# First mixer's projections as matmuls of 512 and 256 columns, halves joined by adding transfers, convolution taps one chunk later

## The chip, the cores and the metric

The kernel runs on one core of one Trainium2 chip, in one launch. Its time is the device time of that core in microseconds (us); a kernel is known by the median of its runs. Engines are named as the profile names them: PE is TensorE (PEld its weight loads), ACT is ScalarE, DVE is VectorE, POOL is GpSimd, SP is SyncE, which only issues transfers here.

## What is computed

The reference is a decoder trunk of two layers over 256 tokens of width 1024. Layer 0 mixes tokens with a Mamba-2 block (SSD), layer 1 with block attention; each is followed by a layer norm, a product-key expert mixer (PEER) over 16384 experts, another layer norm and a gated embedding add. The change is in the first mixer alone. What matters of it:

```python
def ssd_mixer(x, w_in, conv_w, conv_b, dt_bias, a_log, d_skip, norm_g, w_out):
    zxbcdt = x @ w_in                      # 256 x 5152
    z   = zxbcdt[..., :2048]
    xbc = zxbcdt[..., 2048:5120]
    dt  = zxbcdt[..., 5120:]
    xbc = silu(causal_depthwise_conv(xbc, conv_w, conv_b))   # 4 taps along the tokens
    xs, b_in, c_in = xbc[..., :2048], 4 groups of 128, 4 groups of 128
    ...                                    # chunked scan over two chunks of 128 tokens
    gated = y * silu(z)                    # per group of 512 channels
    gated = gated * rsqrt(mean(gated ** 2) + 1e-5)
    return (gated * norm_g) @ w_out
```

All of it is float32, and products are wanted at float32's precision.

## The kernel before

**Products from halves.** A float32 operand is split into a high part that the matrix unit takes exactly and the low rest: ACT writes the high part (`L124`, a cast of 128x1024), DVE the rest (`L125`, a subtraction of the same size). A product then needs three matmuls: high by high, high by low, low by high. `mm3` (`L145` to `L149`) issues these three, each with 256 columns where the tokens move.

**The first mixer's chunks.** The weights come in chunks of 128 output channels: 24 chunks of `w_xbc` (per group g: B, C, four of x), 16 of `w_z`, and 16 chunks of `w_so` for the output. A chunk is a transfer of 512 KB into one of four `raw` buffers, issued by SP, then the cast and the subtraction into one of four `hl` buffers, then the matmuls. `stationary` (`L151`) runs a chunk of `w_xbc` or `w_z` as 8 x 3 matmuls of 256 columns into a PSUM bank of the tag `mm`, of which there are two. The first six chunks of `w_z` are plain float32 matmuls (`L419`) from the unsplit weights and need neither ACT nor DVE first.

**The convolution.** After a chunk of `w_xbc`, `conv` copies the PSUM bank to `cv_raw` on ACT (`L395`), writes `cv_y` as bias plus the last tap on ACT, also from PSUM (`L396`), adds three shifted taps on DVE (`L399`), and applies SiLU on ACT (`L400`). A chunk of `w_z` is copied to `z` (`L423`); SiLU over the four chunks of a group follows later (`L428`).

**The other form of the product, already used elsewhere.** `halves` (`L156` to `L162`) lays the high and the low tokens side by side: a high weight tile meets both in one matmul of 512 columns, whose two halves of the bank are joined afterwards, and a low weight tile meets the high tokens in one of 256. So a chunk has 8 matmuls of each kind; with `turned` the two kinds of weight tile alternate in reversed order, so that two matmuls of one width follow each other. The expert mixer uses it for all 128 chunks of `u`: two ACT copies out of the bank (`L916`, `L917`), and POOL issues a transfer that adds the second copy onto the first (`L918`, 128 KB); the activation that reads the sum comes three to seven chunks later in the program.

**What sets the order.** Each engine runs its own list of instructions in order; a wait at the head of a list holds back everything behind it. The lists are made when the kernel is built, by a scheduler that takes what it holds to be ready, within edges: `after(marks)` keeps an instruction behind a given one on the same engine, and `weave` hands out side work between the chunks. In the first mixer the chunks come as: groups 0 and 1 of `w_xbc` (12 chunks), groups 0 and 1 of `w_z` (8, six of them plain), group 2 of `w_xbc` and the output chunks of group 0, group 3 of `w_xbc` and group 2 of `w_z`, group 3 of `w_z`, the other output chunks. The scan of a group (`ssd_mix`: `L442` to `L518`) and its norm (`L528` to `L540`, where POOL adds squares, `L536`, and takes a root, `L553`) run as side work beside the chunks of later groups.

Of the kernel before, what the change touches and what calls it, by code (L numbers as in the profile page):

```python
# [11 lines left out]
AF = mybir.ActivationFunctionType  # L12
OP = mybir.AluOpType
# [4 lines left out]
P = 128  # L18
T = 256
D = 1024  # L20
KD = D // P
# [19 lines left out]
P_CONVW, P_CONVB, P_D, P_NG, P_LN, P_ALOG, P_DTB, P_END = 0, 96, 120, 136, 152, 216, 248, 280  # L41
# [25 lines left out]
class Net:  # L67
# [88 lines left out]
    def halves(self, out, hl, ks=range(KD), turned=False):  # L156
        o = out.rearrange("p (b t) -> p b t", b=2)
        order = [(k, a) for k in ks for a in ((1, 0) if turned and k % 2 else (0, 1))]
        for k, a in order:
            dst, src = ((o, self.xT[:, :, k, :]), (out[:, :T], self.xT[:, 0, k, :]))[a]  # L160
            self.nc.tensor.matmul(dst, hl[:, a, k * P:(k + 1) * P], src, start=k + a == 0,  # L161
                                  stop=(k, a) == order[-1] and k == KD - 1)  # L162

    def moving(self, out, hl, xk, first, last, c=slice(0, 512)):
        for k in range(2):
# [103 lines left out]
    def ssd(self):  # L269
        nc, dram = self.nc, self.dram  # L270
        with self.tc.tile_pool(name="ssd", bufs=1) as pool:
# [12 lines left out]
            nc.sync.dma_start(self.tri, dram["consts"][:, C_TRI:C_ALIBI])  # L284
            x = pool.tile([P, 2, D], F32, name="xn")
            self.grp, self.zs, self.ns, self.ys, self.ac, self.ce, self.sq, self.rs = ({} for _ in range(8))
            self.last = []
            ins = [self.ssd_in(g) for g in range(4)]
            zs = [self.ssd_z(g) for g in range(4)]
            ssm = [self.ssd_mix(g) for g in range(4)]  # L290
# [96 lines left out]

    def conv(self, dst, hl, c):
        nc, prm = self.nc, self.params
        pc = self.mm()  # L390
        self.stationary(pc[:, :T], hl)
        raw = self.tl([P, T], "cv_raw", 2)
        y = self.tl([P, T], "cv_y", 2)
        w = lambda k: prm[:, P_CONVW + 4 * c + k:P_CONVW + 4 * c + k + 1]
        nc.scalar.copy(raw, pc[:, :T])  # L395
        nc.scalar.activation(y, pc[:, :T], AF.Identity, bias=prm[:, P_CONVB + c:P_CONVB + c + 1], scale=w(3))  # L396
        for k in range(3):
            d = 3 - k
            nc.vector.scalar_tensor_tensor(y[:, d:], raw[:, :T - d], w(k), y[:, d:], op0=OP.mult, op1=OP.add)  # L399
        self.last_silu = nc.scalar.activation(dst, y, AF.Silu).ins  # L400

    def ssd_in(self, g):
        def step(j):
# [7 lines left out]
    def ssd_z(self, g):  # L411
        def step(j):
            if j == 0:
                self.zs[g] = self.tl([P, 4, T], "z", 2)
            pz = self.mm()
            if 4 * g + j in PLAIN:
                raw = self.plain(self.dram["w_z"][4 * g + j])
                for k in range(KD):
                    self.nc.tensor.matmul(pz[:, :T], raw[:, k * P:(k + 1) * P], self.xT32[:, k, :],  # L419
                                          start=k == 0, stop=k == KD - 1)  # L420
            else:
                self.stationary(pz[:, :T], self.chunk(self.dram["w_z"][4 * g + j]))
            self.nc.scalar.copy(self.zs[g][:, j, :], pz[:, :T])  # L423
        return [lambda j=j: step(j) for j in range(4)]

    def ssd_silu(self, g):
# [128 lines left out]
    def ssd_out(self, g, x):  # L555
        def step(kp, h):
            hl = self.chunk(self.dram["w_so"][(2 * g + kp) * 2 + h])
            if kp + h == 0:
                self.oacc = self.accs()
            if g == 3:  # L560
                self.last.append((h, kp, hl, (0, 1)))
                return
            for tb in range(2):
                acc = self.oacc[tb][h]
                self.moving(acc, hl, lambda a, k: self.ns[g][:, a, 2 * kp + k, tb * P:(tb + 1) * P], kp == 0, kp == 1)
                if kp:
                    v = x[:, tb, h * 512:(h + 1) * 512]
                    self.nc.vector.scalar_tensor_tensor(v, acc, self.rs[g][:, tb:tb + 1], v, op0=OP.mult, op1=OP.add)
        return [lambda kp=kp, h=h: step(kp, h) for kp in range(2) for h in range(2)]
# [873 lines left out]
```

## Time and profile before

| | us |
|---|---|
| median of 3 runs | 1862.36 |
| lowest and highest of them | 1859.06, 1872.17 |
| the profiled execution's own time | 1860.15 |
| its span, first to last instruction | 1858.3 |
| PE busy in the span | 1819.4 (98%) |
| DVE busy | 1490.3 (80%) |
| ACT busy | 1151.4 (62%) |
| POOL busy | 635.7 (34%) |

The first mixer takes the first 207 us of the span; the expert mixer of layer 0 begins at 207.35 us. The busy figures are unions over the whole program, whose stages have different limits, so the prediction reads the stretches of the first mixer one by one. In a row of the timeline the first number is the start, the second the length of a run of like instructions, and the bracket tells how long the engine had been idle and who released it. Instructions on one engine overlap a little (the next starts some 0.1 us before the last one's end), so the cost of one in a row of many is read from start to start.

### The profile page before, as it was taken

The page shows a single profiled execution, that of the slowest core. Times are in us where ns is not written, and L with a number is a line of the kernel's source. Part 1 is how long each engine was busy: PE and PEld are TensorE (multiplying, and loading weights), DVE is VectorE, ACT ScalarE, POOL GpSimd, SP SyncE. Part 2 cuts the span into 40 slices and gives each one's busy share as a digit, 9 for nine tenths or more (in the row PEclk, how much of TensorE's full clock was granted, in tenths as well). Part 3 has the DMA queues.
Part 4 walks back from the last instruction along what each step waited for, and adds up shares of the span by engine and source line. Part 5 has one row for each costly group of instructions (what it writes and reads, how often), then busy time and mean ns, then how long its engine had stood idle before and what let it go on. Part 6 is the DMA issues. An engine that isn't in the chain of part 4 may idle for free. (4 is left out here: it accounts for less than half of the span.)

```text
span 1858.3 us, 31744 instructions
## 1 busy us (share of the span) xinstructions
PE 1819.4 (98%) x11112; PEld 1542.1 (83%) x11112; DVE 1490.3 (80%) x2936; ACT 1151.4 (62%) x2330; POOL 635.7 (34%) x620
## 2 busy tenths in 40 slices
PE   9999999999999999999999999999999999999998
PEld 8998888888888877787788788888888887777777
DVE  7798789989989986666667778998998998666656
ACT  6865456696666666555546655669666665555553
POOL 0001013332222257787700001323222225777671
PEclk9999999999999999999999999999999999999999
DMA  7555669897699998889736556989779999888871
GB/s 270 202 186 185 217 178 228 218 243 200 183 275 334 286 313 289 282 291 338 247 107 195 187 195 191 228 217 254 189 185 285 331 288 297 274 279 284 315 238 60
DMA packets 217904, 444.29 MB, mean 239 GB/s; under 512 B 18980, under 2 KB 126664, under 8 KB 216072
## 3 DMA queue, kind: packets, MB, share of 16 engines
q1 hardware_dynamic: 75208, 266.75, 42.8%
q0 software_dynamic: 67648, 137.66, 28.6%
q10 hardware_dynamic: 74880, 37.75, 7.0%
q8 instruction: 91, 1.49, 0.3%
q14 instruction: 77, 0.63, 0.1%
HBM read 364.46 MB, written 44.08 MB: 220 GB/s over the span
## 5 line engine op out<-in xcount | busy, mean ns | idle before, releaser
L125 DVE TENSOR_TENSOR hl<-raw,hl 128x1024 fp32r<-128x1024 f32 x570 | 694.0, 1220 | 205.4 <-ACT hl L124 150.1
L161 PE MATMUL acc<-xT,hl 128*128 128x256 f32 (+1 forms) x4608 | 841.2, 340 | 1.6 <-DVE xT L188 0.8
L161 PEld LDWEIGHTS acc<-xT,hl 128*128 128x128 f32 x4608 | 700.7, 188 | 101.8 <-DVE hl L125 4.2
L124 ACT CAST hl<-raw 128x1024 fp32r<-128x1024 f32 x570 | 597.8, 1052 | 217.2 <-PE acc L149 69.7
L149 PE MATMUL acc<-hl,w 128*128 128x512 f32 x2220 | 529.6, 399 | 27.4 <-issue 9.5
L149 PEld LDWEIGHTS acc<-hl,w 128*128 128x128 f32 x2220 | 423.2, 192 | 132.5 <-issue 18.4
L918 POOL DMA_DIRECT2D w<-w x160 | 139.3, 870 | 399.1 <-ACT w L937 236.5
L918 POOL DMA_DIRECT2D act<-w x96 | 83.7, 872 | 303.6 <-ACT w L917 182.4
L1172 POOL DMA_INDIRECT raw<-in_v,r x136 | 157.9, 1161 | 62.0 <-issue 36.2
L916 ACT COPY w<-acc 128x256 f32<-128x256 f32 x160 | 59.9, 374 | 160.3 <-PE acc L161 156.6
L1172 POOL DMA_INDIRECT rows_w<-w_d,r x122 | 140.0, 1148 | 37.2 <-issue 35.0
L149 PE MATMUL mm<-xT,hl 128*128 128x256 f32 x816 | 100.8, 284 | 0.2 <-DVE hl L125 0.2
L149 PEld LDWEIGHTS mm<-xT,hl 128*128 128x128 f32 x816 | 98.5, 192 | 1.5 <-issue 0.9
L917 ACT COPY w<-acc 128x256 f32<-128x256 f32 x256 | 97.4, 380 | 0.0
L962 DVE TENSOR_TENSOR pick<-pick,r 128x2048 f16<-128x2048 f16 x64 | 78.2, 1222 | 1.0
L978 PEld LDWEIGHTS <-pick 128*128 128x128 f16 x1024 | 67.1, 98 | 13.1 <-issue 9.7
L916 ACT COPY act<-acc 128x256 f32<-128x256 f32 x96 | 35.7, 371 | 66.9 <-PE acc L161 66.4
L979 PE MATMUL mm<-pick 128*128 128x96 f16 x512 | 67.5, 206 | 0.0
L214 POOL TENSOR_TENSOR ln_s<-ln_s,mhalf 128x1 f32<-128x1 f32 x8 | 4.4, 552 | 177.2 <-PE acc L149 130.5
L536 POOL TENSOR_TENSOR sq<-sq,sqt 128x256 f32<-128x256 f32 x12 | 12.5, 1041 | 150.3 <-ACT sqt L535 150.1
L978 PE MATMUL aux<-pick 128*128 128x128 f16 x688 | 59.3, 220 | 0.3
L125 DVE TENSOR_TENSOR hl<-pick,hl 128x1024 fp32r<-128x1024 f32 x32 | 39.2, 1224 | 25.4 <-ACT hl L124 18.9
(290 smaller groups left out, 2118.0 us busy)
## 6 DMA issues: line engine op xcount, KB each, us to landing
raw<-in_u SPq DMA_DIRECT2D x256, 512.0 KB
raw<-in_v SPq DMA_DIRECT2D x64, 512.0 KB
w_d<-act ACTq DMA_DIRECT2D x48, 512.0 KB
w<-w POOLq DMA_DIRECT2D x160, 128.0 KB
raw<-in_w_q SPq DMA_DIRECT2D x32, 512.0 KB
raw<-in_w_xbc SPq DMA_DIRECT2D x24, 512.0 KB
act<-w POOLq DMA_DIRECT2D x96, 128.0 KB
a_d<-act ACTq DMA_DIRECT2D x24, 512.0 KB
```

Source lines behind the costliest of these rows:

```text
L124: a = self.nc.scalar.copy(hi, src)
L125: b = self.nc.vector.tensor_tensor(lo, src, hi.bitcast(F32), op=OP.subtract)
L149: self.last_mm = self.nc.tensor.matmul(out, lhs(a), rhs(b), start=start and i == 0, stop=stop and i == 2).ins
L161: self.nc.tensor.matmul(dst, hl[:, a, k * P:(k + 1) * P], src, start=k + a == 0, stop=(k, a) == order[-1] and k == KD - 1)
L536: nc.gpsimd.tensor_tensor(self.sq[g], self.sq[g], t, op=OP.add)
L916: nc.scalar.copy(whole, pe[:, :T])
L917: copied = nc.scalar.copy(pair[:, 1, :], pe[:, T:]).ins
L918: nc.gpsimd.dma_start(whole, pair[:, 1, :], accum_op=OP.add)
L962: nc.vector.tensor_tensor(a2, both, gates, op=OP.mult)
L978: nc.tensor.matmul(pg[:, t, :], one[:, 0, 4 * h + t], a2[:, 4 * h + t, k], start=k == 0, stop=k == 1)
L979: nc.tensor.matmul(banks["used"][:, MANY * tb:MANY * tb + MANY], one[:, 0, 4 * h + t], a2[:, 4 * h + t, 0, :MANY], start=at == 0, stop=at ...
L1172: got = nc.gpsimd.indirect_dma_start(out=dst, out_offset=None, in_=src, in_offset=rows(which))
```

## The change

Four things change, in the first mixer only.

- The 24 chunks of `w_xbc` and the 10 chunks of `w_z` that are not plain go through `halves` in its turned order: 16 matmuls (8 of 512 columns, 8 of 256) in place of 24 of 256.
- The two halves of the bank are joined as in the expert mixer (`joined`): one ACT copy of the first half into its place (`cv_raw` or `z`), one of the second into a new tile `low`, and a transfer issued by POOL that adds `low` onto it.
- Bias and last tap (`cv_y`) now read `cv_raw` in SBUF, after that transfer, and not PSUM.
- The rest of the convolution of a chunk (`finish`) is put off until after the next chunk's copies: `flush` issues it behind `self.copied`, the last ACT copy. `cv_raw` has three buffers in place of two, `low` has three.

```diff
     def conv(self, dst, hl, c):
         nc, prm = self.nc, self.params
-        pc = self.mm()
-        self.stationary(pc[:, :T], hl)
-        raw = self.tl([P, T], "cv_raw", 2)
-        y = self.tl([P, T], "cv_y", 2)
+        raw = self.tl([P, T], "cv_raw", 3)
+        self.joined(raw, hl)
         w = lambda k: prm[:, P_CONVW + 4 * c + k:P_CONVW + 4 * c + k + 1]
-        nc.scalar.copy(raw, pc[:, :T])
-        nc.scalar.activation(y, pc[:, :T], AF.Identity, bias=prm[:, P_CONVB + c:P_CONVB + c + 1], scale=w(3))
-        for k in range(3):
-            d = 3 - k
-            nc.vector.scalar_tensor_tensor(y[:, d:], raw[:, :T - d], w(k), y[:, d:], op0=OP.mult, op1=OP.add)
-        self.last_silu = nc.scalar.activation(dst, y, AF.Silu).ins
+
+        def finish():
+            y = self.tl([P, T], "cv_y", 2)
+            nc.scalar.activation(y, raw, AF.Identity, bias=prm[:, P_CONVB + c:P_CONVB + c + 1], scale=w(3))
+            for k in range(3):
+                d = 3 - k
+                nc.vector.scalar_tensor_tensor(y[:, d:], raw[:, :T - d], w(k), y[:, d:], op0=OP.mult, op1=OP.add)
+            self.last_silu = nc.scalar.activation(dst, y, AF.Silu).ins
+
+        self.flush()
+        self.pending.append(finish)
+
+    def joined(self, dst, hl):
+        p, low = self.mm(), self.tl([P, T], "low", 3)
+        self.last_mm = self.halves(p, hl, turned=True)
+        self.nc.scalar.copy(dst, p[:, :T])
+        self.copied = self.nc.scalar.copy(low, p[:, T:]).ins
+        self.nc.gpsimd.dma_start(dst, low, accum_op=OP.add)
+
+    def flush(self):
+        while self.pending:
+            with self.after((self.copied,)):
+                self.pending.pop(0)()
...
     def ssd_z(self, g):
...
-                self.stationary(pz[:, :T], self.chunk(self.dram["w_z"][4 * g + j]))
-            self.nc.scalar.copy(self.zs[g][:, j, :], pz[:, :T])
+                self.joined(self.zs[g][:, j, :], self.chunk(self.dram["w_z"][4 * g + j]))
+            self.flush()
...
             if kp + h == 0:
                 self.oacc = self.accs()
+            self.flush()
```

`halves` itself only returns its last matmul now.

First place: ACT's list around the fifth and sixth chunk of `w_xbc`. Before, `mm_302` and `mm_342` are the banks of these chunks, `hl_485` and `hl_532` the split weights of later ones, `xs` the convolution's result.

```order
L395 COPY cv_raw_327<-mm_302 128x256
L396 ACTIVATE cv_y_328<-mm_302,params 128x256
L124 CAST hl_485<-raw_484 128x1024
L400 ACTIVATE xs_131<-cv_y_328 128x256
L395 COPY cv_raw_367<-mm_342 128x256
L396 ACTIVATE cv_y_368<-mm_342,params 128x256
L124 CAST hl_532<-raw_531 128x1024
L400 ACTIVATE xs_131<-cv_y_368 128x256
```

After the change, at the same place, `mm_277`, `mm_312` and `mm_364` are the banks of the fifth, sixth and seventh chunk, and `cv_raw_241` is the fourth chunk's.

```order
L409 COPY cv_raw_276<-mm_277 128x256
L410 COPY low_278<-mm_277 128x256
L124 CAST hl_439<-raw_438 128x1024
L401 ACTIVATE xs_131<-cv_y_263 128x256
L397 ACTIVATE cv_y_298<-cv_raw_241,params 128x256
L409 COPY cv_raw_311<-mm_312 128x256
L410 COPY low_313<-mm_312 128x256
L124 CAST hl_481<-raw_480 128x1024
L397 ACTIVATE cv_y_333<-cv_raw_276,params 128x256
L401 ACTIVATE xs_131<-cv_y_298 128x256
L409 COPY cv_raw_363<-mm_364 128x256
L410 COPY low_365<-mm_364 128x256
```

A chunk's `cv_y` has moved from right behind its own copy to behind the two copies of the next chunk, and ahead of the copies of the one after that; between stand a cast and a SiLU of older chunks.

Second place: DVE's list beside the output chunks of group 0. Before, `cv_y_1152` and `cv_y_1191` are the last two chunks of group 2, and `hl_1234`, `hl_1252`, `hl_1272` the second to fourth output chunk.

```order
L125 TENSOR_TENSOR hl_1234<-raw_1233,hl_1234 128x1024
L399 SCALAR_TENSOR_TENSOR cv_y_1152<-cv_raw_1151,params,cv_y_1152 128x255
L399 SCALAR_TENSOR_TENSOR cv_y_1191<-cv_raw_1190,params,cv_y_1191 128x253
L491 TENSOR_TENSOR ac_477<-ac_477,cbm_1119 128x8x128
L399 SCALAR_TENSOR_TENSOR cv_y_1191<-cv_raw_1190,params,cv_y_1191 128x254
L125 TENSOR_TENSOR hl_1252<-raw_1251,hl_1252 128x1024
L399 SCALAR_TENSOR_TENSOR cv_y_1191<-cv_raw_1190,params,cv_y_1191 128x255
L465 TENSOR_TENSOR xd_1226<-aux_1219,dt_n 128x512
L504 TENSOR_TENSOR ce_479<-ce_479,cf_392 128x1024
L125 TENSOR_TENSOR hl_1272<-raw_1271,hl_1272 128x1024
```

After the change `cv_y_1052`, `cv_y_1086` and `cv_y_1101` are the last three chunks of group 2, and `hl_1152` and `hl_1172` the third and fourth output chunk.

```order
L125 TENSOR_TENSOR hl_1152<-raw_1151,hl_1152 128x1024
L400 SCALAR_TENSOR_TENSOR cv_y_1052<-cv_raw_969,params,cv_y_1052 128x255
L400 SCALAR_TENSOR_TENSOR cv_y_1086<-cv_raw_1030,params,cv_y_1086 128x253
L521 TENSOR_TENSOR ce_433<-ce_433,cf_356 128x1024
L400 SCALAR_TENSOR_TENSOR cv_y_1086<-cv_raw_1030,params,cv_y_1086 128x254
L400 SCALAR_TENSOR_TENSOR cv_y_1101<-cv_raw_1064,params,cv_y_1101 128x253
L400 SCALAR_TENSOR_TENSOR cv_y_1086<-cv_raw_1030,params,cv_y_1086 128x255
L400 SCALAR_TENSOR_TENSOR cv_y_1101<-cv_raw_1064,params,cv_y_1101 128x254
L482 TENSOR_TENSOR xd_1126<-aux_1119,dt_n 128x512
L400 SCALAR_TENSOR_TENSOR cv_y_1101<-cv_raw_1064,params,cv_y_1101 128x255
L125 TENSOR_TENSOR hl_1172<-raw_1171,hl_1172 128x1024
```

The taps of the last two chunks have moved from between the second and third output chunk's subtractions to between the third and fourth, so the fourth now stands behind both.

More of the change, by code (lines that the diff above doesn't have):

```diff
@@ L160, in halves @@
             dst, src = ((o, self.xT[:, :, k, :]), (out[:, :T], self.xT[:, 0, k, :]))[a]
-            self.nc.tensor.matmul(dst, hl[:, a, k * P:(k + 1) * P], src, start=k + a == 0,
-                                  stop=(k, a) == order[-1] and k == KD - 1)
+            last = self.nc.tensor.matmul(dst, hl[:, a, k * P:(k + 1) * P], src, start=k + a == 0,
+                                         stop=(k, a) == order[-1] and k == KD - 1)
+        return last.ins
     def moving(self, out, hl, xk, first, last, c=slice(0, 512)):
@@ L286, in ssd @@
             self.grp, self.zs, self.ns, self.ys, self.ac, self.ce, self.sq, self.rs = ({} for _ in range(8))
-            self.last = []
+            self.last, self.pending = [], []
             ins = [self.ssd_in(g) for g in range(4)]
@@ L414, in step @@
                 self.zs[g] = self.tl([P, 4, T], "z", 2)
-            pz = self.mm()
             if 4 * g + j in PLAIN:
+                pz = self.mm()
                 raw = self.plain(self.dram["w_z"][4 * g + j])
@@ L420, in step @@
                                           start=k == 0, stop=k == KD - 1)
+                self.copied = self.nc.scalar.copy(self.zs[g][:, j, :], pz[:, :T]).ins
             else:
-                self.stationary(pz[:, :T], self.chunk(self.dram["w_z"][4 * g + j]))
-            self.nc.scalar.copy(self.zs[g][:, j, :], pz[:, :T])
+                self.joined(self.zs[g][:, j, :], self.chunk(self.dram["w_z"][4 * g + j]))
+            self.flush()
         return [lambda j=j: step(j) for j in range(4)]
```

## The prediction

> **What bounds the kernel now.** The page's busy line comes first: PE is busy 98% of the span. The change touches only the first mixer, the first 207 us, so the second view is the table of busy time by stretch there, cut where the kinds of chunk change (PE, PEld, DVE, ACT and POOL busy, the granted clock, the transfer engines' share, GB/s).
>
> ```profile
> PE 1819.4 (98%) x11112; PEld 1542.1 (83%) x11112; DVE 1490.3 (80%) x2936; ACT 1151.4 (62%) x2330; POOL 635.7 (34%) x620
> 10.33:47.25 36.92, 36.74 (x299) 35.85 (x299) 34.03 (x88) 27.76 (x52) 0.00 (x0) 1.00 0.78 274
> 47.25:78.87 31.62, 31.62 (x209) 28.26 (x207) 20.06 (x61) 24.85 (x34) 0.00 (x0) 1.00 0.51 175
> 78.87:113.20 34.33, 34.33 (x261) 31.00 (x259) 34.33 (x53) 24.35 (x43) 4.71 (x4) 1.00 0.61 203
> 113.20:147.60 34.40, 34.40 (x309) 33.57 (x307) 32.10 (x51) 22.72 (x45) 3.68 (x4) 1.00 0.58 202
> ```
>
> PE never rests after 10.33 us, at full clock. So PE's own work is what the span is made of, and whatever makes PE wait is added whole. Two things stand close behind: ACT at 27.76 of 36.92 us in the first twelve convolution chunks, and DVE at 34.33 of 34.33 beside group 2 and the first output chunks.
>
> **What the new matmuls take.** PE's timeline has the old form, and ACT's copies in the expert mixer have the new one, since a copy there starts when its chunk's matmuls end.
>
> ```profile
> 29.89 17.52 PE L149 MATMUL mm<-xT,hl 128*128 128x256 f32 x144
> 47.25 3.62 PE L419 MATMUL mm<-xT,raw 128*128 128x256 f32 x16
> 287.82 0.38 ACT L917 COPY w<-acc 128x256 f32<-128x256 f32 x1
> 290.33 0.37 ACT L916 COPY act<-acc 128x256 f32<-128x256 f32 x1 [1.18 <-PE acc L161]
> 290.60 0.38 ACT L917 COPY w<-acc 128x256 f32<-128x256 f32 x1
> 290.87 1.06 ACT L124 CAST hl<-raw 128x1024 fp32r<-128x1024 f32 x1
> 293.12 0.37 ACT L916 COPY act<-acc 128x256 f32<-128x256 f32 x1 [1.19 <-PE acc L161]
> ```
>
> Six old chunks take 47.25 - 29.89 = 17.36 us, 2.89 us each. A new one takes 293.12 - 290.33 = 2.79 us. Both stream 6144 columns, so only some 0.10 us is saved, a tenth of what eight fewer matmuls suggest; over 34 chunks 3.4 us. I take 3.5.
>
> **What is added off PE.** Each of the 34 chunks gets one ACT copy more, 290.87 - 290.60 = 0.27 us from start to start, 9.2 us in all on an engine that idles over 9 us in each of three of the four stretches. `cv_y` from SBUF I cost as from PSUM. DVE's instructions are the same ones, elsewhere. POOL issues 34 transfers at 0.87 us (below), 29.6 us on an engine that has 8.4 busy in these rows. POOL's additions of squares stand among them beside groups 2 and 3:
>
> ```profile
> L536 POOL TENSOR_TENSOR sq<-sq,sqt 128x256 f32<-128x256 f32 x12 | 12.5, 1041 | 150.3 <-ACT sqt L535 150.1
> ```
>
> At 1.04 us each, and waiting on ACT, one or two ahead of a transfer delay it by 1 to 2 us; I cost that at nothing beside the bounds of the transfer's own time, which are 2.6 apart. SP's list keeps its transfers' sequence but for one plain chunk ahead of the decay rows; nothing there waits on the new steps directly.
>
> **The new wait.** This is the term that decides. Before, `cv_y` and the taps waited for a PSUM bank; now they wait for a transfer, and how long one takes from POOL's issue is read from how many packets queue q0, which carries POOL's transfers alone here, moved before the next issue. I read three places: the first such transfer, one in the steady part, and one where the queues are fuller.
>
> ```profile
> 288.49 0.87 POOL L918 DMA_DIRECT2D act<-w  x1 [1.80 <-ACT w L917]
> ...
> q0 software_dynamic: 144, 0.13, 33.2%
> ...
> q0 software_dynamic: 32, 0.03, 7.6%
> q0 software_dynamic: 174, 0.16, 40.3%
> ...
> q0 software_dynamic: 2, 0.00, 0.3%
> q0 software_dynamic: 146, 0.13, 12.1%
> ...
> 285.00:325.00 40.00, 40.00 (x232) 34.89 (x231) 37.94 (x118) 27.27 (x49) 12.50 (x15) 1.00 0.91 224
> ...
> 520.00:600.00 80.00, 80.00 (x650) 69.86 (x649) 69.43 (x108) 48.76 (x146) 19.55 (x23) 1.00 1.10 317
> ```
>
> The first q0 row is the stretch 262.38 to 265.10: one transfer is 144 packets, 0.13 MB, and had landed 2.7 us after its issue. The next two are 288.49 to 291.27 and 291.27 to 293.82: of the transfer issued at 288.49 only 32 packets had moved when the next was issued, 2.8 us on, and the rest by 5.3 us. The last two are 519.45 to 523.54 and 519.45 to 526.31: 2 packets in 4.1 us, all by 6.9 us. The transfer engines' share was 0.91 around the second and 1.10 around the third. POOL starts 0.29 us after `low` is written (290.60 + 0.38 to 291.27, and 287.82 + 0.38 to 288.49). So from the end of `low` to landing, L is 3.0 us at best, up to 5.6 in the steady part, 4.4 to 7.2 with fuller queues. In the first mixer the shares are 0.78, 0.61 and 0.58 without the new transfers; q0's 32.6% for about 16 transfers in 285 to 325 us makes each 0.326 x 40 / 16 = 0.8 us of all sixteen engines, so twelve add 0.26 to the first stretch (to 1.04) and six to ten add 0.14 to 0.24 to the others (to 0.75 and 0.82).
>
> ```profile
> q0 software_dynamic: 2148, 1.95, 32.6%
> ```
>
> The expert mixer hides this landing behind three to seven chunks; here the order of ACT puts `cv_y` of a chunk right behind the next chunk's copies, 2.8 us later, and ahead of the copies of the one after. What ACT has to do from the landing to the end of the copies after it is w: `cv_y`, a cast, a SiLU and two copies.
>
> ```profile
> 25.95 0.42 ACT L400 ACTIVATE xs<-cv_y 128x256 f32<-128x256 f32 x1 [0.58 <-DVE cv_y L399]
> 26.28 0.35 ACT L395 COPY cv_raw<-mm 128x256 f32<-128x256 f32 x1
> 26.53 0.57 ACT L396 ACTIVATE cv_y<-mm,params 128x256 f32<-128x256 f32 x1
> 26.99 1.05 ACT L124 CAST hl<-raw 128x1024 fp32r<-128x1024 f32 x1
> 36.66 1.05 ACT L124 CAST hl<-raw 128x1024 fp32r<-128x1024 f32 x1
> 37.60 0.42 ACT L400 ACTIVATE bf<-cv_y 128x256 f32<-128x256 f32 x1
> ```
>
> That is 0.46 (26.99 - 26.53) + 0.94 (37.60 - 36.66) + 0.33 (26.28 - 25.95) + 0.54 = 2.27 us. A landing and this work together span two chunks, so ACT can keep no shorter period than (L + 2.27) / 2, and PE's 2.79 holds only while L is under 3.3. At the middle of 3.0 and 5.6, L = 4.3, the period is 3.28, 0.49 us a chunk too long. Over the ten of the twelve chunks that have a full predecessor pair this is 4.9 us; the second PSUM bank hides 2.79 - 0.54 = 2.25 of it, once. **First stretch: 2.7 us lost**, from 0 (L = 3.0) to 9.2 (L = 5.6: 3.94, so 10 x 1.15 - 2.25). I take the middle since the share there, 1.04, lies between the rows with 5.3 and 6.9, but ACT's slower pace also thins the weight transfers.
>
> **Second stretch**, 78.87 to 113.20. DVE has no gap there, and the last output chunks' subtractions end just ahead of PE:
>
> ```profile
> 99.49 1.22 DVE L125 TENSOR_TENSOR hl<-raw,hl 128x1024 fp32r<-128x1024 f32 x1
> 102.94 1.22 DVE L125 TENSOR_TENSOR hl<-raw,hl 128x1024 fp32r<-128x1024 f32 x1
> 106.21 2.36 DVE L125 TENSOR_TENSOR hl<-raw,hl 128x1024 fp32r<-128x1024 f32 x2
> 101.84 8.66 PE L149 MATMUL acc<-hl,nhl 128*128 128x512 f32 x36
> 110.43 0.66 PE L514 MATMUL aux<-ac,xd 128*64 128x128 f32 x8
> ```
>
> The 36 matmuls are three chunks of 2.86 us, begun at 101.84, 104.70 and 107.57; their subtractions end at 100.71, 104.16 and 106.21 + 1.22 = 107.43, so 0.14 us are left on the last. The 0.6 us that PE gains on six chunks it then waits for DVE, and each us that DVE waits for a `cv_y` costs one. The fourth output chunk now stands behind the taps of both last chunks. Lower end 0.5 (the six chunks' gain less 0.14), upper end 4.7 (DVE waits for the same landings: six chunks at the 1.15 above, less the 2.25 of the bank). I take 1.5, near the lower end, since the share is only 0.75 here and the subtractions of the fifth and sixth chunk have moved ahead of the first taps. **Third stretch**: six convolution and four z chunks; DVE has 2.3 us free and ACT 11.7; 0 to 2.9 us lost (six chunks at 0.49), I take 0, as the subtractions run ahead again once DVE has gaps, and `z` is not read until its group's SiLU.
>
> **Sum**: -3.5 + 2.7 + 1.5 + 0 = +0.7 us on the profiled execution's own 1860.15 (span 1858.3 and 1.85 around it), so 1860.9. The median of the runs shown, 1862.36, is 2.2 above that execution, so I say 1863. About 1% (18.6 us) is what a measurement of this kernel can tell from no change.
>
> [...]
>
> **Rivals.**
>
> *The gain stands* (30%). A transfer lands within 3.3 us of `low`, as the first one read did, so neither ACT nor DVE waits and only the 3.5 us of PE are seen: 1862.4 - 3.5 = 1859. For it: the share in the later stretches is at or under 0.82, and casts moved ahead of the waits. Against it: the steady rows and DVE's 0.14 us.
>
> *ACT falls behind* (15%). The transfers take as long as around 520 us, L = 7.2 in the first stretch, so the period there is 4.73 and PE loses 10 x 1.94 - 2.25 = 17.2; with 4.7 in the second, less 3.5, +18.4 and 1881, slower. It decides from L = 3.3 up and passes 1% only just above 7.2. For it: 0.26 more share beside 0.78, the four decay-row transfers fall in that stretch. Against it: a period of 4.7 us would halve the weights' demand, and with it L.
>
> *The change is not seen* (in the forecast's part): DVE, which keeps its work, takes all that PE gains; then +0 and 1862.
>
> **Numbers.** The forecast has 55%: 1860 to 1876 (-3.5 + 0 + 0.5 + 0 = -3 up to -3.5 + 9.2 + 4.7 + 2.9 = +13.3 on 1862.36, the likelier part being below 1870). With the rival of 1859 at its lower end the range is 1857 to 1876: the runs before reach 3.3 us below their median, of which I take 2. It leaves out the slow rival. Faster by over 1% needs 18.6 us where 3.5 can be had: 2%. Slower by over 1% is half of the 15%, 7%; within 1% is 91%.
>
> **What would show it.** Chunks of 2.79 us in PE's timeline show the first term right. A wait of ACT at `cv_y` for q0's transfer of 1 to 2 us a chunk, and PE idle for PSUM or `hl` before 60 us, show the second; PE idle near 105 us behind DVE shows the third. If ACT never waits there, the rival of 1859 holds. It is wrong altogether if PE loses time after 207 us.

## The result, and the profile after

The changed kernel takes 1885.36 us (median of 4 runs, 1884.63 to 1893.74) where the kernel before takes 1860.71 (4 runs, 1858.93 to 1872.17). The ratio is 1.0139, with a 95% interval of 1.0110 to 1.0169. It is slower by 1.4%, and 22 us above the forecast of 1863.

The profiled execution of the changed kernel took 1886.06 us, 25.9 more than that of before. These are the busy line of its page and its busy time by stretch, cut at the same events as before: first convolution chunk, first plain chunk of `w_z`, end of the scans of groups 0, 1, 2 and 3, begin of the expert mixer. The columns are PE, PEld, DVE, ACT and POOL busy, granted clock, share of the transfer engines, GB/s.

```profile
PE 1817.9 (96%) x10840; PEld 1528.6 (81%) x10840; DVE 1493.2 (79%) x2936; ACT 1161.1 (62%) x2364; POOL 657.9 (35%) x654
9.70:57.74 48.04, 39.00 (x203) 32.27 (x204) 33.56 (x83) 28.52 (x59) 9.82 (x11) 0.90 0.88 273
57.74:89.54 31.80, 31.80 (x193) 27.64 (x191) 22.13 (x65) 28.25 (x42) 2.59 (x3) 0.99 0.47 141
89.54:128.79 39.25, 35.98 (x214) 29.52 (x212) 34.11 (x54) 26.06 (x49) 9.14 (x10) 0.96 0.70 200
128.79:168.03 39.24, 34.61 (x229) 29.16 (x227) 32.49 (x51) 25.02 (x53) 12.27 (x14) 1.00 0.71 189
168.03:204.46 36.43, 30.57 (x183) 24.38 (x181) 27.27 (x35) 17.81 (x31) 6.89 (x8) 0.95 0.61 187
204.46:235.21 30.75, 30.41 (x141) 24.39 (x140) 25.68 (x46) 17.07 (x28) 6.09 (x6) 1.00 0.50 167
```

The prediction shows four of these stretches of before. The two after them were, in the same view:

```profile
147.60:176.56 28.96, 28.96 (x214) 25.40 (x212) 25.91 (x36) 16.02 (x26) 4.25 (x4) 1.00 0.56 186
176.56:207.35 30.79, 30.44 (x141) 24.41 (x139) 25.67 (x46) 17.08 (x28) 6.10 (x6) 1.00 0.50 168
```

In each row the begin and end of a stretch come first, then its length. The expert mixer begins at 235.21 us in place of 207.35, 27.9 us later; the rest of the program is 1.9 us shorter (1884.3 - 235.21 against 1858.3 - 207.35). So the loss is in the first mixer alone, and two kinds of it can be read from the rows: PE idle (length less PE busy), and PE busy at less than full clock.

| stretch | before | after | lost | more PE idle |
|---|---|---|---|---|
| first: 12 convolution chunks | 36.92 | 48.04 | 11.1 | 8.9 |
| between: first 8 chunks of `w_z` | 31.62 | 31.80 | 0.2 | 0 |
| second: group 2, first output chunks | 34.33 | 39.25 | 4.9 | 3.3 |
| third: group 3, `w_z` of group 2 | 34.40 | 39.24 | 4.8 | 4.6 |
| fourth: `w_z` of group 3, to the end of its scan | 28.96 | 36.43 | 7.5 | 5.9 |
| fifth: up to the expert mixer | 30.79 | 30.75 | 0 | 0 |

What PE waited for, in the view of waits over the whole first mixer (engine, operation, what it waited for: us in total, times, longest), and what ACT waited for there:

```profile
PE mm L161 <- ACT low L410: 15.3, 8, 6.5
...
PE aux L513 <- DVE xd L482: 3.8, 1, 3.8
PE mm L161 <- DVE hl L125: 2.1, 2, 1.3
...
ACT cv_y L397 <- DMA cv_raw<-low: 28.6, 14, 6.8
```

PE waits eight times for a PSUM bank that ACT has not yet emptied. In six of the eight, 12.2 of the 15.3 us, ACT has not emptied it because a `cv_y` ahead of the copies has waited for its transfer, as it does 14 times and up to 6.8 us; the other two, which involve `z`, come below. The longest case, in the timelines of ACT and of PE:

```profile
42.01 0.38 ACT L410 COPY low<-mm 128x256 f32<-128x256 f32 x1
49.20 0.60 ACT L397 ACTIVATE cv_y<-cv_raw,params 128x256 f32<-128x256 f32 x1 [6.81 <-DMA cv_raw<-low]
...
52.02 0.38 ACT L410 COPY low<-mm 128x256 f32<-128x256 f32 x1
...
52.45 5.49 PE L161 MATMUL mm<-xT,hl 128*128 128x512 f32 x16 [6.46 <-ACT low L410]
```

That PE row holds a second loss. The chunk takes 5.49 us, and the clock column tells why (windows of the same profile, the granted clock third from the end):

```profile
45.96:48.17 2.21, 0.02 (x1) 0.00 (x0) 0.00 (x0) 0.00 (x0) 0.00 (x0) 1.00 1.08 380
48.17:52.45 4.28, 0.00 (x1) 0.00 (x1) 2.55 (x10) 2.42 (x7) 0.00 (x0) 0.50 1.03 376
52.45:58.23 5.78, 5.78 (x18) 4.92 (x19) 4.24 (x20) 3.16 (x8) 1.84 (x2) 0.50 0.69 206
...
103.74:105.15 1.41, 0.00 (x1) 0.01 (x1) 0.52 (x2) 1.13 (x3) 0.00 (x0) 1.00 1.04 354
...
106.30:109.62 3.32, 3.32 (x13) 2.79 (x12) 2.96 (x7) 3.32 (x7) 0.00 (x0) 0.50 0.30 60
...
195.00:198.25 3.25, 2.86 (x7) 1.75 (x8) 3.03 (x5) 0.59 (x1) 0.00 (x0) 0.50 0.47 161
```

Three times the clock fell to 0.50 after PE had stood still, and PE then worked 5.78, 3.32 and 2.86 us at that clock. The chunk of 5.49 us takes 1.95 times the 2.81 us of a chunk at 1.00 (five in a row, below), so half of that work, 6.0 us, is lost. More idle (22.6 us, the table's column less rounding) and half clock (6.0), less the gain on PE that is worked out below (3.1 us), make 25.5 of the 28.5 us by which the mixer's stretches grew; the remaining 3 us are not assigned.

### The profile page after: what moved, and what is told of

The parts are those of the page before. It is cut to its first block, busy times and chain, and to the rows that moved or that the text cites. A ratio compares the mean times of both kernels' runs of the same rounds, so it can differ in the third digit from the quotient of the medians.

```text
span 1884.3 us, 31402 instructions
## 1 busy us (share of the span) xinstructions
PE 1817.9 (96%) x10840; PEld 1528.6 (81%) x10840; DVE 1493.2 (79%) x2936; ACT 1161.1 (62%) x2364; POOL 657.9 (35%) x654
## 4 chain that ended last, share of the span: by engine, by line
PE 43%; DVE 5%; issue 3%; POOL 2%; DMA 2%; ACT 2%; another core or an unknown queue 1%; ACTq 0%; DVEq 0%; POOLq 0%
PE acc L149 19%; PE acc L161 18%; PE mm L161 2%; DVE hl L125 1%; PE aux L996 1%; POOL raw L1190 1%; DMA pick<-in_v,r 1%; ACT hl L124 1%; DMA raw<-in_v,r 1%; POOL pick L1190 1%; POOL rows_w L1190 1%; PE mm L997 1%; PE mm L996 0%; PE mm L186 0%
## 5 line engine op out<-in xcount | busy, mean ns | idle before, releaser
L149 PE MATMUL acc<-hl,w 128*128 128x512 f32 x2220 | 521.5, 395 | 28.9 <-issue 12.0
L1190 POOL DMA_INDIRECT raw<-in_v,r x136 | 153.6, 1129 | 71.3 <-issue 32.5
L161 PE MATMUL mm<-xT,hl 128*128 128x512 f32 (+1 forms) x800 | 153.0, 348 | 17.9 <-ACT low L410 15.3
L161 PEld LDWEIGHTS mm<-xT,hl 128*128 128x128 f32 x800 | 125.1, 193 | 42.1 <-ACT low L410 18.3
L1190 POOL DMA_INDIRECT rows_w<-w_d,r x122 | 137.3, 1126 | 37.2 <-issue 36.3
L1190 POOL DMA_INDIRECT pick<-a_d,r x46 | 52.2, 1136 | 19.3 <-issue 13.1
```

The costliest lines, as they stand in the source:

```text
L149: self.last_mm = self.nc.tensor.matmul(out, lhs(a), rhs(b), start=start and i == 0, stop=stop and i == 2).ins
L161: last = self.nc.tensor.matmul(dst, hl[:, a, k * P:(k + 1) * P], src, start=k + a == 0, stop=(k, a) == order[-1] and k == KD - 1)
L1190: got = nc.gpsimd.indirect_dma_start(out=dst, out_offset=None, in_=src, in_offset=rows(which))
```

## The experiments

They ran on three other chips, on which the kernel before was run again beside them: 1836.03 us for the first four, 1835.84 for the next four, 1859.51 for the last three. So only ratios and lengths of stretches are compared. The theories: **A**, ACT and all behind it wait for the landing of the adding transfer. **B**, the added transfers hold up the other transfers, whether anyone waits for them or not. **C**, the new order of ACT and DVE costs time by itself. The table has for each kernel the ratio to the kernel before, the lengths of the mixer's stretches in us, and the time at which the expert mixer begins.

| kernel | ratio, 95% interval | first | between | second | third | fourth | expert mixer at |
|---|---|---|---|---|---|---|---|
| before | | 36.9 | 31.6 | 34.3 | 34.4 | 29.0 | 207.4 |
| changed | 1.0139, 1.0110 to 1.0169 | 48.0 | 31.8 | 39.3 | 39.2 | 36.4 | 235.2 |
| joined by DVE | 1.0039, 1.0020 to 1.0058 | 36.8 | 31.8 | 40.8 | 34.1 | 28.8 | 213.5 |
| deferred only | 0.9985, 0.9962 to 1.0008 | 36.6 | 32.2 | 34.1 | 34.4 | 29.0 | 207.8 |
| transfers only | 1.0024, 1.0001 to 1.0047 | 39.6 | 31.7 | 34.1 | 35.7 | 30.9 | 212.8 |
| two chunks later | 1.0113, 1.0059 to 1.0166 | 37.6 | 37.5 | 44.7 | 34.8 | 34.6 | 230.1 |
| `w_z` only | 1.0063, 1.0040 to 1.0086 | 37.3 | 31.5 | 36.5 | 34.1 | 35.5 | 215.1 |
| `w_xbc` only | 1.0103, 1.0073 to 1.0134 | 47.5 | 31.7 | 37.9 | 39.8 | 29.0 | 227.0 |
| small decay rows | 1.0169, 1.0137 to 1.0201 | 49.2 | 31.4 | 39.3 | 39.0 | 32.4 | 231.8 |
| sum unread | 1.0019, 0.9994 to 1.0044 | 36.3 | 32.5 | 33.7 | 33.7 | 31.2 | 207.7 |
| other rows | 1.0151, 1.0123 to 1.0179 | 46.4 | 34.1 | 39.5 | 39.8 | 33.0 | 233.7 |
| no rows | 1.0143, 1.0112 to 1.0174 | 40.6 | 34.1 | 39.4 | 38.9 | 32.4 | 226.3 |
| DVE, not group 2 | 1.0011, 0.9986 to 1.0037 | 37.4 | 31.8 | 35.3 | 35.3 | 29.8 | 210.7 |

**Halves joined by DVE, no transfer.** The new matmuls stay; the high half is added from PSUM to `low` by DVE, and the convolution is not put off.

```diff
-        self.nc.scalar.copy(dst, p[:, :T])
         self.copied = self.nc.scalar.copy(low, p[:, T:]).ins
-        self.nc.gpsimd.dma_start(dst, low, accum_op=OP.add)
+        self.nc.vector.tensor_tensor(dst, p[:, :T], low, op=OP.add)
...
-        self.flush()
-        self.pending.append(finish)
+        finish()
```

> The matmuls of 512 and 256 columns alone: the halves are joined by one ACT copy and one addition on DVE out of PSUM, at once, with no transfer and nothing put off. Theory A (ACT stands in its list until an adding transfer has landed, and PE then waits for its PSUM bank or its weights): 0 to 3.5 us faster than the kernel before, since no landing is waited for; up to 3 us of it can go to the 34 new DVE additions of some 0.42 us where DVE has no gap. Theory B (the traffic of the transfers costs, waited for or not): the same. Theory C (putting the taps off starves the lists by order alone): the same. If the new matmuls are themselves slower than read, this kernel is slower than before by 5 us or more under none of the three.

It was slower by 0.4%, so the expected gain was a miss. All of the loss is in the second stretch, where DVE had no gap to begin with; the others are 0.1 to 0.3 us shorter, but for one that is 0.2 longer. Its waits of PE in that stretch, and the stretch:

```profile
PE mm L161 <- DVE hl L125: 3.3, 2, 2.8
PE aux L561 <- POOL sq L551: 1.5, 1, 1.5
...
78.97:119.80 40.83, 35.99 (x213) 29.42 (x211) 38.14 (x61) 25.18 (x43) 3.93 (x4) 0.96 0.57 185
```

PE stood still for 40.83 - 35.99 = 4.8 us, and the clock of 0.96 shows that here too it fell. But without the landing the first stretch is whole again: A holds there so far, C and B are still possible.

**Deferred only.** The old matmuls and one copy; no second copy, no transfer; the rest of the convolution one chunk later as in the change.

```diff
-        p, low = self.mm(), self.tl([P, T], "low", 3)
-        self.last_mm = self.halves(p, hl, turned=True)
-        self.nc.scalar.copy(dst, p[:, :T])
-        self.copied = self.nc.scalar.copy(low, p[:, T:]).ins
-        self.nc.gpsimd.dma_start(dst, low, accum_op=OP.add)
+        p = self.mm()
+        self.stationary(p[:, :T], hl)
+        self.copied = self.nc.scalar.copy(dst, p[:, :T]).ins
```

> The putting off alone: three matmuls of 256 columns as before, one ACT copy of the result, bias and taps one chunk later from that copy, no halves and no transfer. Theory A: within 2 us of the kernel before. Theory B: the same. Theory C: most of the 25 us are lost here too, 10 or more.

The ratio is 0.9985, no change, and no stretch is over 0.6 us longer. The order alone costs nothing: C falls.

**Transfers only.** The kernel before, and for each of the 34 chunks one ACT copy into `low` and one adding transfer onto a tile that nobody reads.

```diff
+    def idle_add(self, p):
+        low = self.tl([P, T], "low", 4)
+        self.nc.scalar.copy(low, p[:, :T])
+        self.adds += 1
+        self.nc.gpsimd.dma_start(self.sums[:, self.adds % 4, :], low, accum_op=OP.add)
...
```

> The kernel before, with one more ACT copy per chunk and an adding transfer of 128 KB per chunk from POOL into a tile that nobody reads: all the added copies and transfers, at the same places, with nothing waiting for a landing. Theory A: 0 to 4 us slower than the kernel before (9 us more on ACT beside other work, some weights later). Theory B: 15 to 25 us slower. Theory C: 0 to 4 us slower.

The ratio is 1.0024, 4.4 us and so just over what A expected, and the expert mixer begins 5.4 us later. So B has a share: the copies of `low`, the transfers and their load cost about a fifth of the 27.9 us at most.

**Sum unread.** The change with one line altered: the transfer adds onto a tile that nobody reads, so `cv_y` and SiLU wait for ACT's own copy alone, and the part from the low tokens is left out of the sums.

```diff
-        self.nc.gpsimd.dma_start(dst, low, accum_op=OP.add)
+        self.adds += 1
+        self.nc.gpsimd.dma_start(self.sums[:, self.adds % 4, :], low, accum_op=OP.add)
```

> The change with all its matmuls, copies, transfers and its putting off, but each transfer adds the second half onto a tile that nobody reads, and the convolution and z go on from the first half alone (the products of the low tokens are left out of the result, nothing else is). So the work is the change's, and only the wait for the landing is gone. Theory A (that wait costs the time): 0 to 6 us slower than the kernel before, of which the traffic's 4.4 us measured by themselves are the most part; the first mixer ends 22 us or more earlier than in the change. Theory B (something else in the change costs it, the new matmuls or the added work together): 15 us slower or more.

With the matmuls, both copies, the transfers and the order of the change in place, and only the wait gone, the expert mixer begins at 207.7 us, within 0.4 of before, and the ratio is 1.0019. Its second and fourth stretch:

```profile
78.39:112.08 33.69, 33.69 (x213) 28.23 (x211) 33.59 (x53) 26.03 (x49) 10.22 (x10) 1.00 0.81 230
145.73:176.89 31.16, 29.15 (x182) 23.54 (x180) 26.92 (x35) 17.41 (x30) 7.66 (x8) 1.00 0.69 211
```

PE is not idle in the second stretch, DVE, which has hardly a gap there, keeps pace, and the clock is full. A is shown: the 27.9 us come from waiting for the landing and from what that brings with it. It also shows that little was to be had: the gain on PE goes in part into the 2.0 us of 31.16 that PE is idle in the fourth stretch.

**`w_z` only and `w_xbc` only.** In the first, the convolution chunks are as before the change; in the second, the ten chunks of `w_z`.

```diff
-                self.joined(self.zs[g][:, j, :], self.chunk(self.dram["w_z"][4 * g + j]))
+                pz = self.mm()
+                self.stationary(pz[:, :T], self.chunk(self.dram["w_z"][4 * g + j]))
+                self.copied = self.nc.scalar.copy(self.zs[g][:, j, :], pz[:, :T]).ins
```

> The change for the 10 z chunks alone; the convolution as before. Theory A: only SiLU over z waits for a landing, with the casts behind it in ACT's list: 4 to 9 us slower than the kernel before, nearly all of it after 147 us of the span. If z's wait costs nothing by itself, within 1 us.

> The change for the 24 convolution chunks alone; z by three matmuls of 256 columns and one copy, as before. Theory A: the waits at the convolution cost the first three stretches their 10.5, 4.9 and 4.8 us, the z wait before the fourth its 7.5; so 15 to 21 us slower than the kernel before, with the fourth stretch at its old 29 us.

They split the loss by place: the expert mixer begins 7.7 us later with `w_z` alone changed and 19.6 with `w_xbc` alone, together 27.3 of the 27.9. With `w_z` alone changed the fourth stretch is 35.5 us (29.0 before), with `w_xbc` alone it is 29.0; the first, 37.3 and 47.5. The fourth stretch's loss therefore belongs to `z`, which the prediction cost at nothing. `z` also costs in the second stretch, 2.2 us with `w_z` alone, where nearly all was expected after 147 us. There the changed kernel's timelines of ACT and of PE name the transfer:

```profile
93.45 1.07 ACT L445 ACTIVATE z<-z 128x1024 f32<-128x1024 f32 x1 [2.44 <-DMA z<-low]
...
96.50 5.85 PE L161 MATMUL mm<-xT,hl 128*128 128x512 f32 x32 [1.11 <-ACT low L410]
```

SiLU over `z` of group 1 waits for the landing, the copies that empty the next bank stand behind it, and PE waits 1.1 us. What happens in the fourth stretch, in the timelines of ACT and DVE:

```profile
185.13 0.37 ACT L410 COPY low<-mm 128x256 f32<-128x256 f32 x1
185.40 2.00 ACT L124 CAST hl<-raw 128x1024 fp32r<-128x1024 f32 x2
190.80 1.06 ACT L445 ACTIVATE z<-z 128x1024 f32<-128x1024 f32 x1 [3.40 <-issue]
191.76 1.03 ACT L124 CAST hl<-raw 128x1024 fp32r<-128x1024 f32 x1
...
192.82 1.23 DVE L125 TENSOR_TENSOR hl<-raw,hl 128x1024 fp32r<-128x1024 f32 x1 [2.77 <-ACT hl L124]
194.56 0.68 DVE L482 TENSOR_TENSOR xd<-aux,dt_n 128x512 f32<-128x512 f32 x1
```

SiLU over `z` stands two casts behind the last chunk's copies. It waits for the last landing, and the cast behind it is late; DVE's subtraction waits for that cast, `xd` stands behind the subtraction, and PE waits 3.8 us for `xd` (the row among the waits above). The profile names "issue" for this wait of ACT and not the transfer. But by q0's packets the last transfer, issued at 185.80 us, landed at 190.41, 0.4 us before SiLU starts; and in the kernel with the sum unread SiLU over `z` follows the last copy at once:

```profile
160.94 0.37 ACT L413 COPY low<-mm 128x256 f32<-128x256 f32 x1
161.20 1.07 ACT L449 ACTIVATE z<-z 128x1024 f32<-128x1024 f32 x1
```

The other 2.1 us that PE stands still in the fourth stretch, at 175.95, are for a bank. They are only in part the wait of `z`: ahead of the copies ACT had waited 3.1 us for a weight transfer of the expert mixer and then 1.1 us for the landing of group 2. Why that weight came late was not followed.

**Two chunks later.** The rest of the convolution is put off by two chunks, with four buffers each for `cv_raw` and `low`.

```diff
-        raw = self.tl([P, T], "cv_raw", 3)
+        raw = self.tl([P, T], "cv_raw", 4)
...
-        while self.pending:
+        self.tick += 1
+        while self.pending and self.tick - self.pending[0][0] >= 2:
...
```

> The change with the convolution put off by two chunks in place of one (four buffers for the copies in place of three); z as in the change. Theory A: landings of up to 5.6 us after the copy now fit into two chunks, so the first three stretches give back 12 to 20 of their 20 us; the waits of z's SiLU stay: 3 to 12 us slower than the kernel before. Theory B: still 20 to 25 us slower. Theory C: 20 us slower or more, as more is put off.

The first stretch came back to 37.6 us and the third to 34.8, as A expects of a wait that is given 2.8 us more, though landings in the first took up to 9.7 us by q0's packets. But the ratio was 1.0113, well above what was expected, since two other stretches paid:

```profile
64.59 1.89 ACT L468 ACTIVATE ac<-ac 128x2048 f32<-128x2048 f32 x1
66.39 0.62 ACT L438 COPY z<-mm 128x256 f32<-128x256 f32 x2
...
66.79 1.65 PE L436 MATMUL mm<-xT,raw 128*128 128x256 f32 x3 [2.48 <-ACT z L438]
...
104.66 1.01 PE L564 MATMUL aux<-ones,sq 128*128 128x2 f32 x4 [4.55 <-POOL sq L554]
```

The last SiLU of the convolution ends later, so the block of exponentials of the decays, kept behind it, lands between the plain chunks and ACT's copies of them, and PE waits 2.5 us for a bank. In the second stretch PE waits 4.6 us for squares that POOL adds. So in this one run more lag moves the waits; in this order of work it does not remove them.

**What makes landings long.** In the changed kernel, the transfers issued by POOL at 40.37 and 42.68 us land 8.4 and 9.3 us later: between the two issues queue q0 moved nothing, and from 42.68 to 51.96 both (288 packets are two transfers). The queue rows of these two windows:

```profile
q1 hardware_dynamic: 122, 0.86, 88.8%
...
q1 hardware_dynamic: 442, 3.17, 83.6%
q0 software_dynamic: 288, 0.26, 17.6%
```

At that time the four transfers of decay rows (1 MB each in SBUF) are on q1, the queue of SP's transfers. Three kernels ask whether they are the cause. In the first, one head's row stands for all eight, and an eighth of the bytes moves.

```diff
-        self.nc.sync.dma_start(ac, self.rows[8 * g:8 * g + 8].rearrange("(o h) (c l) -> o h c l", o=1, c=2)
-                               .to_broadcast([P, 8, 2, P]))
+        one = self.one[g] = self.tl([P, 1, 2, P], "one", 4)
+        self.nc.sync.dma_start(one, self.rows[8 * g:8 * g + 1].rearrange("(o h) (c l) -> o h c l", o=1, c=2)
+                               .to_broadcast([P, 1, 2, P]))
...
```

> The change with the four broadcast transfers of decay rows (1 MB each) cut to an eighth: one head's row stands for all eight, so the decays of the other heads are left out, and no arithmetic instruction is. If the queue of these 4 MB is what stretched the landings to 8 and 9 us at 40 to 52 us, the 6.8 us wait of ACT there goes and the first stretch falls from 48.0 to 39 to 43 us: 5 to 9 us faster than the change, 16 to 20 us slower than the kernel before. If the weight transfers alone do it, the first stretch stays at 46 to 48 us.

In the second, the same bytes come from 128 different rows of the weights.

```diff
-        self.nc.sync.dma_start(ac, self.rows[8 * g:8 * g + 8].rearrange("(o h) (c l) -> o h c l", o=1, c=2)
-                               .to_broadcast([P, 8, 2, P]))
+        for k in range(2):
+            self.nc.sync.dma_start(ac[:, 4 * k:4 * k + 4], self.dram["w_z"][2 * g + k].rearrange("p (h c l) -> p h c l", h=4, c=2))
```

> The changed kernel, but the four decay tiles are filled with rows of the weights of z (as many bytes, 128 different rows in memory) in place of one row read by all 128 partitions; the decays are therefore wrong. If it is the reading of one row 128 times that holds queue q0 back while the landings take 8 to 9 us (36 to 45 us in the span), those landings fall to 3 to 5 us here, the longest wait of cv_y (6.8 us) to under 3, the first stretch to 41 to 44 us (48.0 in the changed kernel) and the ratio to the kernel before to 1.009 to 1.012. If the bytes queued on q1 do it, or the descriptors of POOL, landings of 8 us remain, the first stretch stays at 46 to 49 us and the ratio at 1.013 to 1.017.

In the third, there is no such transfer.

```diff
-        self.nc.sync.dma_start(ac, self.rows[8 * g:8 * g + 8].rearrange("(o h) (c l) -> o h c l", o=1, c=2)
-                               .to_broadcast([P, 8, 2, P]))
+        if not self.one:
+            one = self.tl([P, 1, 2, P], "one", 1)
+            self.nc.vector.memset(one, -1.0)
+            self.one = {k: one for k in range(4)}
...
```

> The changed kernel without the four transfers of decay rows at all: one small tile set once to a constant stands for all rows, so the decays are wrong. If those transfers (their row, or their place on SP ahead of the weights) stretch the landings, no landing before 58 us takes over 6 us, the first stretch is 40 to 43 us and the ratio to the kernel before 1.006 to 1.011. If the landings are stretched by weights and plain z chunks on q1 alone, landings of 8 us remain at about 40 us, the first stretch is 46 to 49 us and the ratio 1.013 to 1.017.

ACT's wait for the landings up to 62 us in the changed kernel and in these three, in that order (the first row of the same view of each):

```profile
ACT cv_y L397 <- DMA cv_raw<-low: 15.4, 6, 6.8
```

```profile
ACT cv_y L397 <- DMA cv_raw<-low: 15.5, 6, 7.3
```

```profile
ACT cv_y L397 <- DMA cv_raw<-low: 14.9, 8, 4.2
```

```profile
ACT cv_y L397 <- DMA cv_raw<-low: 6.4, 7, 1.5
```

Fewer bytes change nothing: the transfers issued at 41 and 44 us still take 9.7 and 8.6 us to land there, and the first stretch is 49.2 us. With other rows, SP issues two of the four loads at 16.8 to 19.7 us and two at 36.4 to 39.0, and the long landings are the ones right behind them: 7.8 and 7.4 us for the transfers issued at 18.3 and 23.7, 6.7 and 6.3 for those at 40.7 and 44.0. Without the transfers no landing of the first stretch takes over 5.0 us, and ACT's wait falls from 15.4 to 6.4 us. First stretch and the one between are counted together here, because without the rows a plain chunk runs ahead of the last convolution chunk: 68.5 us before, 79.8 changed, 80.6, 80.5 and 74.7 in the three. So the transfers of decay rows make 5.1 of the 11.3 us that these two stretches lose, and the expected 40 to 43 us for the first stretch and no landing over 6 held. The time did not follow: with a ratio of 1.0143 this kernel can't be told from the changed one, though its mixer ends 8.9 us earlier. And 4.0 of the 8.9 us are not from the missing transfers: the fourth stretch is 32.4 to 33.0 us in all three kernels, against 36.4, as the last landing there takes 2.3 to 2.4 us in them and 4.6 in the changed kernel; why was not followed. By which property the transfers of decay rows hold up q0 stays open: it is neither the bytes nor the one row alone.

**Joined by DVE, but not in group 2.** The kernel joined by DVE, with the six chunks of group 2 as before the change.

```diff
+        if c in (8, 9, 10, 11, 18, 22):
+            p = self.mm()
+            self.stationary(p[:, :T], hl)
+            src = p[:, :T]
+            self.copied = nc.scalar.copy(raw, src).ins
+        else:
+            self.joined(raw, hl)
+            src = raw
...
-            nc.scalar.activation(y, raw, AF.Identity, bias=prm[:, P_CONVB + c:P_CONVB + c + 1], scale=w(3))
+            nc.scalar.activation(y, src, AF.Identity, bias=prm[:, P_CONVB + c:P_CONVB + c + 1], scale=w(3))
...
```

> As the kernel with the halves joined by a DVE addition from PSUM, but the six chunks of group 2 keep the old matmuls of 256 columns and their old convolution. If the 6.5 us lost there came from six more additions on a DVE without a gap, the third stretch is back at 34.0 to 34.6 us, the other stretches keep their 0.1 to 0.3 us each, and the time is 0.3 to 1.5 us under the kernel before (ratio 0.999 to 1.000). If the additions cost wherever they stand, or the loss in that stretch came from what goes before it, the time is 3 to 8 us above it (ratio 1.002 to 1.004).

(That text counts the stretch between as the second; its third is the second here.) The second stretch is 35.3 us where it was 40.8, so the new form of these six chunks, with its six more additions on a full DVE, made 5.5 of the 6.5 us lost there. The other stretches did not keep their gain (35.3 and 29.8 us in the third and fourth, 34.1 and 28.8 in the kernel joined by DVE), and the ratio, 1.0011, is no change. No version that was run beats the kernel before.

## Why the prediction was wrong

It forecast 1863 us, 1857 to 1876, and the time is 1885. The mechanism that it named first, `cv_y` waiting for the landing ahead of the copies that free PE's bank, is the one that the kernel with the sum unread shows. What failed: the size of the first stretch, the step on `z`, DVE as what PE would wait for in the second stretch, and two terms left out, the clock and the chunks after 147.6 us.

- **The gain on PE** (-3.5) was right. Five chunks in a row, before and after, in PE's timeline:

```profile
113.20 14.64 PE L149 MATMUL mm<-xT,hl 128*128 128x256 f32 x120
127.68 0.61 PE L474 MATMUL aux<-cf,bf 128*128 128x128 f32 x4
```

```profile
128.79 14.21 PE L161 MATMUL mm<-xT,hl 128*128 128x512 f32 x80
142.83 0.61 PE L491 MATMUL aux<-cf,bf 128*128 128x128 f32 x4
```

  That is 2.90 and 2.81 us a chunk, and 34 x 0.09 = 3.1 us.

- **The first stretch** (2.7, bounds 0 and 9.2) lost 11.1 net, so 12.2 with the gain of twelve chunks put back. The term was mis-sized. It took one L of 4.3 us for every chunk, with 5.6 as the upper end. The twelve landings counted from q0's packets took 2.3 to 9.3 us from issue, with a mean of 4.7, so L was 5.0 in the mean, for which the same formula gives 10 x 0.85 - 2.25 = 6.2. Of the rest, 6.0 us, 2.9 are the clock (half of the 5.78 at half speed); the other 3.1 can be put down to the two landings of over 8 us, which made one wait of 6.81, but no run separates them. The prediction saw that the four decay-row transfers fall in this stretch, but put that with the slow rival and not into L; without them the loss of this stretch and the one between is 6.2 of 11.3 us. Its reason against that rival, that ACT's slower pace would thin the other transfers and so shorten L, held in the mean but not where it mattered. With the sum unread, where ACT keeps its pace, the share in the stretch is 0.96 and the twelve landings take 6.2 us in the mean; here they are 0.88 and 4.7. But the two longest take as long here (8.4 and 9.3, against 8.8 and 9.1), and the share was 1.03 to 1.08 in the windows above in which PE stood still for them. (A slip in the share's own sum: 2148 packets are 14.9 transfers of 144, not 16, so each is 0.87 us of all sixteen engines and not 0.8.)

- **The clock** has no term. Every wait was costed at its own length. The 5.78 + 3.32 + 2.86 us at half clock cost 6.0 us more, a fifth of the loss. When it falls is not told by the length of a wait alone: at 48.17 it fell 2.2 us into a wait of PE of 6.46, at 195.00 3.4 us into one of 3.79, and at 106.30 after one of 1.42, when PE had been at work again for 1.15 us; but PE also stood still for 2.13 us before 157.88 and for 2.07 before 175.95, and the clock stayed at 1.00. What decides between them no run shows.

- **The second stretch** (1.5, bounds 0.5 and 4.7) lost 4.9 net, 5.4 with the gain put back, of which 1.7 is the clock. Without that, at 3.7, it is inside the bounds, but in part by luck. The prediction had PE wait for DVE there, and of the 3.3 us that PE stood still only 0.7, at 123.25, were for DVE. Another 1.1 were behind SiLU over `z`, which was costed at nothing, and 1.4, at 105.15, behind a `cv_y`. The reason for staying near the lower end, the smaller share of the transfer engines, did not hold: the share was 0.70, below the 0.75 expected, and still two landings took 5.5 and 6.6 us and ACT waited 3.66.

```profile
103.96 0.60 ACT L397 ACTIVATE cv_y<-cv_raw,params 128x256 f32<-128x256 f32 x1 [3.66 <-DMA cv_raw<-low]
```

- **The third stretch** (0, bounds 0 and 2.9) lost 4.8 net. At its beginning five chunks ran at full pace in spite of the waits, as the row of 14.21 us shows. After them PE stood still 4.6 us: 3.3 for banks, of which 2.1 behind a wait of ACT of 3.1, and 1.3 for DVE's subtraction. That subtractions run ahead once DVE has gaps, the reason for costing it at nothing, held for those five chunks only.

```profile
155.75 0.60 ACT L397 ACTIVATE cv_y<-cv_raw,params 128x256 f32<-128x256 f32 x1 [3.11 <-DMA cv_raw<-low]
...
157.88 3.30 PE L161 MATMUL mm<-xT,hl 128*128 128x512 f32 x17 [2.13 <-ACT low L410]
```

- **"`z` is not read until its group's SiLU"** is the step that was wrong, and not only in size. It is true, but it says nothing of when that SiLU comes. The trace of before had the answer:

```profile
161.31 0.35 ACT L423 COPY z<-mm 128x256 f32<-128x256 f32 x1
161.56 1.05 ACT L124 CAST hl<-raw 128x1024 fp32r<-128x1024 f32 x1
162.51 1.06 ACT L428 ACTIVATE z<-z 128x1024 f32<-128x1024 f32 x1
```

  SiLU over `z` starts 1.2 us after the last copy, with any landing the prediction read (2.7 us at least) far longer. And the prediction stopped at 147.6 us, where it had cut its table, while four of the ten changed chunks of `w_z` lie behind that. This missing stretch is 7.5 of the 27.9 us; of the 5.9 us that PE stood still there, 3.8 are behind the SiLU of group 3 and 2.1 are the mixed wait above.

- **The rivals.** The slow one, ACT falling behind, at 15% and 1881 us, was the nearest. Its place and its price were partly right: it expected 17.2 us from the first stretch, by landings of 7.2 us throughout, and 4.7 from the second. 11.1 and 4.9 came from there, and 12.3 from the third and fourth, which it left at nothing; so its total, near the measured one, is partly luck. The rival by which the gain stands would not have come true even without the wait: with the sum unread, the ratio is 1.0019.

- **The edits costed at nothing** held: deferring the taps (0.9985), and mostly the second copy, POOL's issues and the load of the transfers (1.0024).

## What to carry to other kernels

Here a wait for a transfer at the head of an engine's list cost most where the landings were longest (8.4 and 9.3 us), and a middle value (4.3) undersized it, so look for what else is queued in that stretch and size the wait by it; a transfer that elsewhere hides behind three to seven chunks was not free one chunk ahead of its reader (ACT waited 28.6 us for it in all). For each result that now arrives later, find the time at which its first reader starts in the trace, through to the last changed chunk, before calling it hidden. Where PE is the bound, a wait can cost more than its length: here three waits, the shortest of 1.4 us, cost another 1.4 to 2.9 us each through the clock.

## What was not expected of the hardware

By q0's packets, a 128 KB adding transfer landed 2.3 us after its issue at best and 9.7 at worst, in the first stretch of the kernel with small decay rows; the three that the prediction read had landed by 2.7, 5.3 and 6.9 us. In that kernel the two longest landings were under way while the other queue moved little and q0 nothing. The other queue's row from 42 to 48 us (packets, MB, share of the sixteen engines):

```profile
q1 hardware_dynamic: 390, 0.44, 27.9%
```

So these long landings did not need transfer engines that are busy on the average of the sixteen (28% here), and their share, by which the prediction sized L, was not enough to size them by. The view does not part the sixteen, so whether a single one was full stays open.
